# A streaming encoder layer on one core: where split weights start in their buffers, and the order of the opening's splits

## The chip, the cores and the metric

One core of a Trainium2 chip runs the whole layer in one launch. The metric is the device time in microseconds (us), the median of three runs. TensorE multiplies, VectorE and ScalarE do elementwise work, GpSimd small parts; DMA transfers are issued from an engine's queue, here nearly all from the sync engine (SP).

## The reference

One layer of a hybrid encoder over 2048 prompt tokens and 8 x 16 sample tokens, model width 1024, all in float32. Cut to what matters here:

```python
qm, km, vm, om, ip, fp, qa, ka, va = split_in(x @ w_in)          # input projection
hm = mlstm_chunkwise(...)                                        # 4 heads x 128
ha = swa_prompt(...) or swa_step(...)                            # windowed attention
mix = jnp.concatenate([hm, ha], axis=-1) @ w_out                 # output projection
h = layer_norm(DEEPNORM_ALPHA * x + mix, ln1_g, ln1_b)
u = h @ w_up                                                     # up product, 2 x 2816 wide
c = b_conv + sum(ext[:, j:j + T] * w_conv[j] for j in range(CONV_W))
a, g = jnp.split(c, 2, axis=-1)
y = layer_norm(DEEPNORM_ALPHA * h + (silu(g) * a) @ w_down, ln2_g, ln2_b)   # down product
```

## The kernel before, in words

Every large product is made in split precision: each operand is cast on ScalarE to a high part and the rest is subtracted on VectorE to a low part (`split`, L219: a cast at L221, a subtraction at L222). Three matmuls, high x high, high x low and low x high, then stand for one. The input, up and down products also use a seven-product scheme for 2 x 2 blocks: sums and differences of the quarters of weights and tokens are multiplied, products 1 to 7. The sums of tokens are called t1 to t4 in `x_steps` (L551), and a digit there is the split of that product's tokens.

The stages follow each other on TensorE. The input projection (`i_dense`, L599) goes over four blocks of 512 prompt tokens, the first with the sample tile beside it. `i_direct` (L735, matmuls at L747) makes keys, values and gates with narrow weights, `i_product` (L709, L721) one of the seven products for one of five groups of columns: 24 matmuls of 256 columns. In groups 0 and 1 the weights are the stationary operand and tokens move; in groups 2 to 4 the tokens are stationary and weights move. The sample tile's own products are at L731. The recurrence and the attention of finished blocks are woven between these matmuls as chains (`Chains`, L155 on). The output projection (`group`, L917, through `mm3`, L224 to L228) has tokens stationary and 512 columns of weights moving. The up product (`f_product`, L887, matmuls at L1895) has weights stationary and 384 or 320 tokens moving; the down product (`f_downs`, L2076, matmuls at L2103) has tokens stationary and 512 columns of weights moving.

The order on TensorE is written out by hand: `i_begin` (L346) lists the items of the input projection, and `i_dense` yields them with costs, by which the chains are woven in. For the first block the list begins with the gates of tiles 0 to 3, then product (block 0, group 0, 1), the gates of the sample tile, and (0,0,2), (0,1,1), (0,0,7), (0,0,6), (0,0,5), (0,0,4), (0,0,3). The other engines take their instructions in the order in which the program asks for them, with a priority for evictions.

Split weights stand in a ring of buffers: four with the tag `wlo`, four with `whi` (`WB = 4`), and two more, `wex`, from the second stage on. `half` (L398) gives one of them to the input and output projections, `f_slot` (L1782) to the up and down products. `advance` (L422) asks for as many splits (`next_split`, L472) and loads (`next_raw`, L431) as there are free buffers. A buffer's bytes in each partition begin where the pools put it: a pool lays its tiles out one after the other, each rounded up to 32 bytes, and a pool begins where the one before it ends. The largest tile of a tag sets the size of its buffers; the gates' tile of 2 x 2 x 272 floats makes it 4352 bytes, 17 x 256, for `wlo` and `whi`. `pad` (L216) takes some bytes of a pool to move what follows. By these sizes the first weight buffer begins at byte 1728, which is 192 past a multiple of 256, and all buffers of the ring do the same modulo 256, `wex` by its pad. Split tokens begin at a multiple of 256, and those of the down product, which `f_buf` (L1776) places 56 floats into their buffers, at 224 past one.

The opening is the part of `i_dense` ahead of its loop. It loads the tokens of block 0 in four quarters (`x_load`, L542; quarter 1 in two pieces), gate weights and the sample tile, all on the sync queue, warms TensorE up with products of zeros (`warm_up`, L326), then asks for the splits of gate weights and tokens. `x_steps(0, 1)` splits the first quarter in four pieces. Ahead of the loop it asks for all seven token operands of block 0 but product 4's.

## Time and profile before

| what | value |
| --- | --- |
| median of 3 runs | 2289.33 us (2288.55 to 2289.89) |
| profiled execution | 2291.27 us, its span 2289.5 us, mean granted TensorE clock 0.999 |
| instructions | 39775, of which 14293 matmuls |
| DMA | 631.30 MB, mean 276 GB/s |
| HBM | 457.02 MB read, 171.64 MB written |
| input projection, matmuls at L721 | first at 20.6 us, last at 613.6 us |
| output projection, L228 | 615.5 to 893.8 us |
| up product, L1895 | 894.2 to 1817.7 us |
| down product, L2103 | 1818.3 to 2280.7 us |

How to read it: the span runs from the first to the last instruction of one profiled execution. A row of the timeline gives start, length, engine, line, operation, output<-inputs and shapes; a matmul's inputs are named moving operand first, then the stationary one, and "x2" puts two that follow each other into one row. A matmul's length is drawn from its start to its modelled end, and matmuls are pipelined, so the distance between two starts is shorter than the length. The bracket at a row's end is the idle time of the engine before it and who ended it. Idle time of an engine other than the one that sets the end costs nothing.

### The profile page before, as it was taken

Reading aid. Unit: us, or ns where it says so; the run is one execution under the profiler, and the core shown is the slowest. Engines: PE = TensorE matmul, PEld = TensorE weight load, DVE = VectorE, ACT = ScalarE, POOL = GpSimd, SP = SyncE. Lnnn points to the kernel's source line nnn. Section 1 sums busy time; section 2 is a strip of 40 time slices with the busy share of each in tenths; the row PEclk is TensorE's granted clock in tenths of the full one; section 3 lists DMA queues with packets and bytes.
Section 4 is the critical chain, followed back from the end, with each engine's and each line's share of the span. In section 5 each row is a group of like instructions: output and inputs, shape, how many; then the busy total and the mean of one; then the engine's idle time right before and its main releaser. Section 6 shows DMA issues by size and latency. Waiting matters only on the chain. (4 is left out here: it accounts for less than half of the span.)

```text
span 2289.5 us, 39775 instructions
## 1 busy us (share of the span) xinstructions
PE 2269.4 (99%) x14293; PEld 2083.6 (91%) x14293; DVE 1808.9 (79%) x3068; ACT 1272.9 (56%) x2373; POOL 275.5 (12%) x509
## 2 busy tenths in 40 slices
PE   8999999999999999999999999999999999999998
PEld 8999999999878778999999999999999988888876
DVE  8787687777688888998778777778766786995987
ACT  5453476776766656555556555555555644444442
POOL 0001001000021110211112000113111200200200
PEclk9999999999999999999999999999999999999999
DMA  7989998899998867898778999988998786757752
GB/s 280 321 313 317 319 317 275 276 308 298 329 315 266 270 217 273 310 328 302 285 272 272 307 305 311 307 269 290 323 288 262 253 291 227 252 164 223 251 157 84
DMA packets 302133, 631.30 MB, mean 276 GB/s; under 512 B 47404, under 2 KB 140656, under 8 KB 301936
## 3 DMA queue, kind: packets, MB, share of 16 engines
q1 hardware_dynamic: 297264, 615.06, 79.5%
q0 software_dynamic: 3520, 10.56, 1.5%
q10 hardware_dynamic: 1152, 3.15, 0.4%
q8 instruction: 113, 1.85, 0.3%
q14 instruction: 84, 0.69, 0.1%
HBM read 457.02 MB, written 171.64 MB: 275 GB/s over the span
## 5 line engine op out<-in xcount | busy, mean ns | idle before, releaser
L1895 PE MATMUL fup<-hh,uw 128*128 128x384 f32 (+1 forms) x1848 | 476.9, 327 | 0.2 <-ACT ub L1924 0.2
L1895 PE MATMUL dps<-hh,uw 128*128 128x384 f32 (+1 forms) x1848 | 476.7, 327 | 0.0
L1895 PEld LDWEIGHTS fup<-hh,uw 128*128 128x128 f32 x1848 | 329.1, 188 | 0.5 <-ACT ub L1924 0.4
L1895 PEld LDWEIGHTS dps<-hh,uw 128*128 128x128 f32 x1848 | 329.1, 188 | 0.0
L1895 PE MATMUL fup<-hl,uw 128*128 128x384 f32 (+1 forms) x924 | 301.9, 327 | 1.0 <-DVE hl L222 1.0
L1895 PE MATMUL dps<-hl,uw 128*128 128x384 f32 (+1 forms) x924 | 301.6, 326 | 0.0
L1953 DVE SCALAR_TENSOR_TENSOR cc<-u,cw,cc 128x768 f32<-128x768 f32 (+1 forms) x264 | 258.0, 978 | 38.6 <-ACT cc L1951 30.2
L221 ACT CAST uw<-wraw 128x1024 fp32r<-128x1024 f32 x126 | 123.6, 981 | 229.0 <-PE dps L2103 122.5
L721 PE MATMUL dps<-w,oh 128*128 128x256 f32 x1344 | 250.3, 282 | 0.4 <-ACT dps L815 0.4
L222 DVE TENSOR_TENSOR w<-wraw,w 128x1024 fp32r<-128x1024 f32 (+2 forms) x163 | 186.1, 1149 | 61.8 <-ACT w L221 60.4
L221 ACT CAST w<-wraw 128x1024 fp32r<-128x1024 f32 (+2 forms) x163 | 160.3, 992 | 112.6 <-PE dps L721 58.3
L721 PEld LDWEIGHTS dps<-w,oh 128*128 128x128 f32 x1344 | 209.5, 188 | 11.5 <-issue 8.1
L222 DVE TENSOR_TENSOR uw<-wraw,uw 128x1024 fp32r<-128x1024 f32 x126 | 142.3, 1129 | 61.7 <-ACT uw L221 61.2
L721 PE MATMUL dps<-w,ol 128*128 128x256 f32 x672 | 186.8, 278 | 0.0
L1895 PEld LDWEIGHTS fup<-hl,uw 128*128 128x128 f32 x924 | 173.6, 188 | 1.7 <-DVE hl L222 1.6
L721 PE MATMUL dps<-oh,w 128*128 128x256 f32 x896 | 170.7, 284 | 3.8 <-DVE w L222 2.2
L2103 PE MATMUL fup<-uw,fu 128*128 128x512 f32 x726 | 173.8, 396 | 0.0
L1895 PEld LDWEIGHTS dps<-hl,uw 128*128 128x128 f32 x924 | 173.6, 188 | 0.0
L2103 PEld LDWEIGHTS fup<-uw,fu 128*128 128x128 f32 x726 | 136.4, 188 | 33.0
L2103 PE MATMUL dps<-uw,fu 128*128 128x512 f32 x660 | 165.0, 396 | 0.0
L2103 PEld LDWEIGHTS dps<-uw,fu 128*128 128x128 f32 x660 | 124.0, 188 | 30.0
L721 PEld LDWEIGHTS dps<-oh,w 128*128 128x128 f32 x896 | 140.5, 188 | 10.1 <-issue 4.1
(320 smaller groups left out, 4565.1 us busy)
## 6 DMA issues: line engine op xcount, KB each, us to landing
uw<-zw SPq DMA_DIRECT2D x176, 512.0 KB, 5.1
zw<-uw SPq DMA_DIRECT2D x88, 512.0 KB, 3.3
w<-zws SPq DMA_DIRECT2D x72, 512.0 KB, 6.3
wv<-wup SPq DMA_DIRECT2D x66, 512.0 KB, 5.4
wraw<-wi SPq DMA_DIRECT2D x65, 512.0 KB, 5.1
wraw<-zt SPq DMA_DIRECT2D x60, 512.0 KB, 4.6
wraw<-wdn SPq DMA_DIRECT2D x45, 512.0 KB, 4.9
wraw<-wo SPq DMA_DIRECT2D x40, 512.0 KB, 4.9
```

The costliest lines, as they stand in the source:

```text
L221: nc.scalar.copy(hi, src)
L222: return nc.vector.tensor_sub(lo, src, hi.bitcast(F32)).ins
L721: mm(o, l, r, start=s in (1, 7) and c == k == i == 0, stop=k == 3 and i == 2, skip_group_check=True)
L1895: mm(ps, l[:, k], r[:, k], start=s in (1, 7) and k == 0 and i == 0, stop=k == 3 and i == 2, skip_group_check=True)
L1953: V.scalar_tensor_tensor(c[:, v], u[:, i:i + n], w[i], c[:, v], op0=ALU.mult, op1=ALU.add)
L2103: mm(ps, l[:, k, c], r[:, k], start=s in (1, 4, 7) and u == 0 and k == 0 and i == 0, stop=u == nu - 1 and k == n - 1 and i == 2, skip_grou ...
```

## The change

It has two parts.

The first is where split weights begin. Every slot of the ring is now one tile of 1088 floats (`WS`, 4352 bytes), and the caller says at which float its data begin: `half(at, size)` and `f_slot(at)`. The offset is 16 floats (64 bytes) for groups 0 and 1 of the input projection, 48 floats (192 bytes) for groups 2 to 4 and for the up product, 0 for the gates, the output projection and the down product. A pad of 64 bytes in the first pool moves the ring's first buffer to byte 1792, a multiple of 256. The pads of the pools behind it are dropped, one of 192 bytes is added in `f_downs`, and `f_buf` is gone: the token buffers of the up and down products begin at their tiles' start, which by the sizes is again a multiple of 256.

The second is the opening's order. The load of the first raw gate weights and of token quarter 1 is asked for ahead of the warm-up; quarters 1 and 3 go in two pieces each and are issued from ScalarE's queue. The second token operand is split in two pieces, with a split of gate weights after each (`between`). Of the sums and splits of tokens only t3 and 7 stay ahead of the loop; t2 and 6 are asked for after the gates of the sample tile, t1 and 5 after product (0,0,2), t4, 4 and the sample tile's operand 4 after (0,1,1).

```diff
@@ -36,6 +36,7 @@
 
 WB = 4
 WR = 7
+WS = 1088
 
 
 IBLOCKS = [[0, 1, 2, 3, 16], [4, 5, 6, 7], [8, 9, 10, 11], [12, 13, 14, 15]]
@@ -248,11 +249,12 @@
             chains = Chains(self)
             self.xs, self.gates, self.i_done = {}, {}, 0
             self.i_begin()
+            self.next_raw()
+            self.x_load(0, 1)
             self.warm_up()
             chains.weave(self.i_dense())
             close(mcm)
             wx, wxcm = enter("wx1sb")
-            self.pad(wx, 192)
             self.unit_more(wx)
             self.mp, mcm = enter("osb")
             self.o_setup()
@@ -287,9 +289,7 @@
             close(xcm)
 
             self.wx, wxcm = enter("wx2sb")
-            self.pad(self.wx, 192)
             self.f2, f2cm = enter("f2sb")
-            self.pad(self.f2, 64)
             self.f3, f3cm = enter("f3sb")
             self.pad(self.f3, 192)
             self.pad(self.fp, 224)
@@ -310,6 +310,7 @@
         nc.vector.memset(self.eps, EPS)
         self.mhalf = cp.tile([P, 8], F32, name="mhalf")
         nc.vector.memset(self.mhalf, -0.5)
+        self.pad(cp, 64)
         self.zqk = [dp.tile([8, P, P * len(b)], F32, name=f"zqk{i}") for i, b in enumerate(IBLOCKS)]
         self.zws = [[dp.tile([1 if g < KEPT else 2, P, 4, HT], F32, name=f"zws{g}_{i}") for i in range(4)] for g in range(NG)]
         self.zo = [[dp.tile([len(b), P, 512], F32, name=f"{n}{i}") for i, b in enumerate(IBLOCKS)] for n in ("zqa", "zog", "zv")]
@@ -395,15 +396,15 @@
     def release(self, n):
         self.halves[1] += n
 
-    def half(self, shape):
+    def half(self, at, size):
         n = self.halves[0]
         self.halves[0] += 1
         if self.extra is not None:
             e = (n - self.extra) % (2 * WB + 2)
             if e < 2:
-                return self.wx.tile(shape, F32R, name="w", tag="wex", bufs=2)
+                return self.wx.tile([P, WS], F32R, name="w", tag="wex", bufs=2)[:, at:at + size]
         self.turn = 1 - self.turn
-        return self.wp.tile(shape, F32R, name="w", tag=("wlo", "whi")[self.turn], bufs=WB)
+        return self.wp.tile([P, WS], F32R, name="w", tag=("wlo", "whi")[self.turn], bufs=WB)[:, at:at + size]
 
     def unit_more(self, wx):
         self.wx, self.extra = wx, self.halves[0]
@@ -480,12 +481,13 @@
         self.us += 1
         if u[0] == "g":
             e = self.raw_of.pop(u)
-            w = self.half([P, 2, 2, 272])[:, :, :, :264]
+            w = self.half(0, WS).rearrange("p (i k m) -> p i k m", i=2, k=2)[:, :, :, :264]
             self.split(w[:, 0], w[:, 1], e[0])
             e[1] = True
             self.wu[u] = w[:, 0], w[:, 1]
             return True
-        hi, lo = self.half([P, 1024]), self.half([P, 1024])
+        at = 0 if u[0] == "o" else 16 if u[2] < 2 else 48
+        hi, lo = self.half(at, 1024), self.half(at, 1024)
         if self.kept(u):
             for i, t in enumerate((hi, lo)):
                 self.nc.sync.dma_start(t.bitcast(F32), self.zws[u[2]][SUMS.index(u[3])][i].rearrange("p a b -> p (a b)"))
@@ -543,12 +545,13 @@
         for q in qs:
             self.xr[b, q] = r = self.x_raw(q)
             x = self.a["xq"][b][(q - 1) // 2, (q - 1) % 2]
-            n = 2 if (b, q) == (0, 1) else 1
+            first = b == 0 and q in (1, 3)
+            n = 2 if first else 1
             for i in range(n):
                 k = slice(i * 4 // n, (i + 1) * 4 // n)
-                self.nc.sync.dma_start(r[:, k], x[:, k])
-
-    def x_steps(self, b, *steps):
+                (self.nc.scalar if first else self.nc.sync).dma_start(r[:, k], x[:, k])
+
+    def x_steps(self, b, *steps, between=None):
 
         nc, V = self.nc, self.nc.vector
         r = lambda q: self.xr[b, q]
@@ -571,11 +574,13 @@
                 x = self.xt[0] if s in (7, 6) else r({1: 1, 2: 3, 3: 4, "b12": 2, 5: 2, 4: 4}[s])
 
                 self.hx[b, s] = h, l = self.x_slot(4 if s == "b12" else s)
-                n = 4 if (b, s) == (0, 1) else 1
+                n = 4 if (b, s) == (0, 1) else 2 if (b, s) == (0, 2) else 1
                 for i in range(n):
                     k = slice(i * 4 // n, (i + 1) * 4 // n)
                     nc.scalar.copy(h[:, k], x[:, k])
                     V.tensor_sub(l[:, k], x[:, k], h[:, k].bitcast(F32))
+                    if between:
+                        between()
 
     def x_single(self, *steps):
@@ -601,8 +606,6 @@
         nb = len(IBLOCKS)
         last = NG - 1
 
-        self.next_raw()
-        self.x_load(0, 1)
         self.next_raw()
         self.x_load(0, 3)
         for _ in range(2):
@@ -617,16 +620,12 @@
         self.next_split()
         self.x_steps(0, 1)
         self.next_split()
-        self.x_steps(0, 2)
-        for _ in range(2):
-            self.next_split()
+        self.x_steps(0, 2, between=self.next_split)
         self.x_steps(0, "b12", 3)
         self.x_single(1, 2)
         self.next_raw()
         self.advance()
-        self.x_steps(0, "t3", 7, "t2", 6)
-        self.x_single(4)
-        self.x_steps(0, "t1", 5, "t4")
+        self.x_steps(0, "t3", 7)
         self.sb, self.trans = {}, None
 
         passages = [{1: ["load"], 7: ["t3", 7], 6: ["t2", 6], 2: [1], 5: [2], 3: [3, "t4"], 4: ["b12", "t1"]},
@@ -662,10 +661,11 @@
                 self.i_keys(b, ti, ps)
                 if ti == 3 and b or ti == 4:
                     self.release(4)
-                    self.x_steps(b, 4)
                     if b:
-                        self.x_steps(b, 5)
+                        self.x_steps(b, 4, 5)
                 self.advance()
+                if ti == 4:
+                    self.x_steps(0, "t2", 6)
                 continue
             _, b, g, s = item
             if item not in self.wu:
@@ -695,6 +695,11 @@
                 self.x_pair(0, (7, 5, 2, 3).index(s))
             with self.tc.issue_after(behind) if behind and b == 0 else nullcontext():
                 self.advance()
+            if (b, g, s) == (0, 0, 2):
+                self.x_steps(0, "t1", 5)
+            elif (b, g, s) == (0, 1, 1):
+                self.x_steps(0, "t4", 4)
+                self.x_single(4)
 
             if (b, g) in ((1, 1), (nb - 2, 1), (nb - 1, 0), (nb - 1, 2)):
@@ -1719,7 +1724,7 @@
 
             n = len(tiles) // 2
             for ts, tags in ((range(n), ("hh6", "hl6")), (range(n, 2 * n), ("hh7", "hl7"))):
-                w = [self.f_buf(fp, F32, "hst", tag, [3, 512]) for tag in tags]
+                w = [fp.tile([P, 3, 512], F32, name="hst", tag=tag, bufs=1) for tag in tags]
                 for c, t in enumerate(ts):
                     z = self.zh[tiles[t]].rearrange("p (i m) -> p i m", i=2)
                     at = [((2 * c + i) // 3, (2 * c + i) % 3) for i in range(2)]
@@ -1769,21 +1774,18 @@
                 V.tensor_sub(r3, r3, r2)
             else:
                 pool = self.fp if s in (1, 7, 6) else self.f3 if s == 4 else self.f2
-                hi, lo = [self.f_buf(pool, F32R, f"{n}{s}", f"{n}{s}", [4, 384]) for n in ("hh", "hl")]
+                hi = pool.tile([P, 4, 384], F32R, name=f"hh{s}", tag=f"hh{s}", bufs=1)
+                lo = pool.tile([P, 4, 384], F32R, name=f"hl{s}", tag=f"hl{s}", bufs=1)
                 self.split(hi[:, :, :h], lo[:, :, :h], src[s])
                 self.hc[b, s] = hi[:, :, :h], lo[:, :, :h]
 
-    def f_buf(self, pool, dt, name, tag, shape, at=0):
-
-        t = pool.tile([P, 1536 + (64 if pool is self.fp else 0)], dt, name=name, tag=tag, bufs=1)[:, at:at + 1536]
-        d = dict(zip("abc", shape[:-1]))
-        return t.rearrange(f"p ({' '.join(d)} m) -> p {' '.join(d)} m", **d)
-
-    def f_slot(self, dt=F32R):
+    def f_slot(self, at, dt=F32R):
         self.slot = (self.slot + 1) % 10
         if self.slot < 8:
-            return self.wp.tile([P, KD, P], dt, name="uw", tag=("whi", "wlo")[self.slot % 2], bufs=WB)
-        return self.wx.tile([P, KD, P], dt, name="uw", tag="wex", bufs=2)
+            w = self.wp.tile([P, WS], dt, name="uw", tag=("whi", "wlo")[self.slot % 2], bufs=WB)
+        else:
+            w = self.wx.tile([P, WS], dt, name="uw", tag="wex", bufs=2)
+        return w[:, at:at + D].rearrange("p (k m) -> p k m", k=KD)
 
     def f_raw(self, b, j):
@@ -1808,7 +1810,7 @@
                 self.f_raw(b, j)
             if b == 0:
                 v, g = self.wr[b, j]
-                s12, s34 = self.f_slot(F32), self.f_slot(F32)
+                s12, s34 = self.f_slot(48, F32), self.f_slot(48, F32)
                 V.tensor_add(s12[:, :4], g[:, :4], g[:, 4:])
                 V.tensor_sub(s34[:, :4], v[:, :4], g[:, :4])
                 V.tensor_sub(s12[:, 4:], s12[:, :4], v[:, :4])
@@ -1816,7 +1818,7 @@
                 self.wr[b, j] = v, g, s12, s34
         if s == 5 and (b, j) != (len(FBLOCKS) - 1, NFF - 1):
             self.f_raw(b + (j + 1) // NFF, (j + 1) % NFF)
-        w = self.f_slot().rearrange("p (i k) m -> p i k m", i=2)
+        w = self.f_slot(48).rearrange("p (i k) m -> p i k m", i=2)
         i = SUMS.index(s) if s in SUMS else None
         keep = None if i is None else self.zw[j][i].rearrange("p (i k m) -> p i k m", i=2, k=4)
         if b and i is not None:
@@ -2038,7 +2040,7 @@
         src = src[k0 + ks[0]:k0 + ks[-1] + 1, :, c0:c0 + 512].rearrange("k p n -> p k n")
         n = len(ks) * 512
         raw = self.wp.tile([P, 1024], F32, name="wraw", tag="wraw", bufs=WR)
-        hi, lo = [self.f_slot().rearrange("p a b -> p (a b)") for _ in range(2)]
+        hi, lo = [self.f_slot(0).rearrange("p a b -> p (a b)") for _ in range(2)]
         v = lambda t: t[:, :n].rearrange("p (a b) -> p a b", b=512)
         self.nc.sync.dma_start(v(raw), src)
         self.low = self.split(hi[:, :n], lo[:, :n], raw[:, :n])
@@ -2055,7 +2057,7 @@
         ks = slice(DUNITS[u][0], DUNITS[u][-1] + 1)
         n = len(DUNITS[u])
         r = {q: self.dr[b, q][:, ks, :h] for q in (1, 2, 3, 4) if (b, q) in self.dr}
-        w = self.f_buf(self.fp, F32R, "fu", ("hh1", "hl1", "hh7", "hl7", "hh6", "hl6")[self.ring % 6], [2, 2, 384], 56)
+        w = self.fp.tile([P, 2, 2, 384], F32R, name="fu", tag=("hh1", "hl1", "hh7", "hl7", "hh6", "hl6")[self.ring % 6], bufs=1)
         self.ring += 1
         if s == 6:
             V.tensor_sub(r[1], r[4], r[1])
@@ -2090,6 +2092,7 @@
         nb, nu = len(FBLOCKS), len(DUNITS)
         ys, ops = {}, {}
         last_tile = FBLOCKS[-1][0]
+        self.pad(self.wp, 192)
         st = self.wp.tile([P, 2, 6], F32, name="st", tag="st", bufs=1)
 
         def product(s, p, units):
```

## The prediction

> **What bounds the kernel now.** I read the page first, then the windows of the opening, the timeline of PE there, and last the timeline of PE stage by stage for the distance from one matmul's start to the next.
>
> ```profile
> span 2289.5 us, 39775 instructions
> PE 2269.4 (99%) x14293; PEld 2083.6 (91%) x14293; DVE 1808.9 (79%) x3068; ACT 1272.9 (56%) x2373; POOL 275.5 (12%) x509
> ```
>
> TensorE is busy for 2269.4 of 2289.5 us and its instructions stand in an order written out by hand. So there are two things to win: the 20.1 us in which it is idle, and the distance between matmuls that follow each other without a gap. The second isn't in the busy time (a matmul is drawn longer than its distance to the next); it is read from starts. The change aims at both: the opening's order at the first, the byte offsets at the second.
>
> ```profile
> 0.00:6.00 6.00, 4.02 (x10) 3.13 (x10) 2.99 (x13) 2.63 (x4) 0.31 (x5) 1.00 0.60 176
> 6.00:18.70 12.70, 11.28 (x82) 10.48 (x81) 9.31 (x17) 8.21 (x17) 0.00 (x0) 1.00 1.03 408
> 18.70:50.00 31.30, 28.40 (x234) 27.59 (x233) 31.12 (x53) 16.16 (x26) 0.00 (x0) 1.00 0.72 249
> ```
>
> These are windows of the opening (stretch, length, busy PE, PEld, DVE, ACT, POOL, then clock, DMA share, GB/s). Until 6 us the DMA engines are busy for only 0.60 of the time; then they are full to 18.7 us (1.03, 408 GB/s); from there to 50 us VectorE works 31.12 of 31.30 us. First the loads, then VectorE, set the pace.
>
> ```profile
> 8.28 0.39 PE L747 MATMUL dps<-w,oh 128*128 128x264 f32 x1 [0.73 <-ACT w L221]
> 9.02 0.39 PE L747 MATMUL dps<-w,oh 128*128 128x264 f32 x1 [0.36 <-DVE w L222]
> ...
> 11.81 0.39 PE L747 MATMUL dps<-w,oh 128*128 128x264 f32 x1 [0.34 <-DVE w L222]
> ...
> 33.66 0.50 PE L721 MATMUL dps<-oh,w 128*128 128x256 f32 x2 [1.30 <-DVE w L222]
> ...
> 41.83 0.50 PE L721 MATMUL dps<-oh,w 128*128 128x256 f32 x2 [0.91 <-DVE w L222]
> ...
> 45.37 0.39 PE L721 MATMUL dps<-oh,w 128*128 128x256 f32 x1 [0.69 <-ACT zev L787]
> ```
>
> These are PE's idle times in the opening after its first real product (the bracket is the idle time and who ended it): 0.73 + 0.36 + 0.34 = 1.4 us for the first splits, 1.30 + 0.91 = 2.2 us for weight splits of VectorE, 0.69 us for an eviction.
>
> **The change, the opening.** VectorE's queue ahead of the wait that ends at 33.66 us:
>
> ```profile
> 23.90 1.22 DVE L569 TENSOR_TENSOR xr<-xr 128x1024 f32<-128x1024 f32 x1
> ...
> 27.44 1.22 DVE L578 TENSOR_TENSOR ol<-xr,oh 128x1024 fp32r<-128x1024 f32 x1
> ...
> 29.92 1.22 DVE L565 TENSOR_TENSOR xr<-xr,xt 128x1024 f32<-128x1024 f32 x1
> ...
> 32.39 1.22 DVE L222 TENSOR_TENSOR w<-wraw,w 128x1024 fp32r<-128x1024 f32 x1
> ```
>
> The split at 32.39 is the one that PE waits for (it ends at 33.6). Ahead of it stand the sum t1 (23.90), the split of tokens 5 (27.44) and the sum t4 (29.92), all for products (0,0,5) to (0,0,4), which come after the product that waits. The change asks for t1 and 5 after product (0,0,2), for t4 and 4 after (0,1,1), and for t2 and 6 after the single tile: 3 x 1.22 = 3.7 us leave the queue ahead of the split, t2 and 6 perhaps too. The wait is 1.30 us, so it goes, and I take the 0.91 us at 41.83 to go as well: there the same three steps are still ahead less t4, some 2.4 us, and PE comes 1.3 us earlier. What is late next is the deferred work itself: t1, 5, t4 and 4 are 4 x 1.22 = 4.9 us, to be done between (0,1,1) and (0,0,4), while VectorE has no idle time to give. Their cover is the queue of split weights that stands ahead of PE (four units of two halves); gone, it costs at most the 2.2 us that were won. The 0.69 us stays: product (0,0,5) needs the bank that (0,0,6) has just filled.
>
> The loads of tokens 1 and 3 go in halves by ScalarE's queue, so the sync queue has three issues fewer ahead of the gate weights and the first weights (the halves of 1, and 3 whole). Below 6 us the DMA engines have 0.40 of their time free, 2.4 us of full rate; what is issued earlier there also lands earlier. Bounds for the 1.4 us of first waits: all of it, and nothing if the landing of the first tokens stays put; the free 2.4 us exceed it, so I take it all. The four issues lie on ScalarE, which before its first cast does a table load alone and then sits idle until tokens land; they are covered there, and if they aren't, the first cast is late by what sticks out. Tokens 2 in two pieces cost two more small operations, covered by VectorE's idle time from 6 to 18.7 us (9.31 busy of 12.70). Opening: 3.6 us won, between 0 and 5.
>
> **The change, the offsets.** From the tile sizes in the code (each rounded up to 32 bytes): before, all split weights stand at 192 bytes past a multiple of 256, split tokens at 0, and tokens of the down product at 224. After, weights stand at 64 in groups 0 and 1 of the input projection, at 192 in groups 2 to 4 and in the up product, and at 0 in the gates, the output projection and the down product, whose tokens come to 0. The other tokens stay at 0. So the address pairs change in groups 0 and 1 (weights stationary, 192 to 64), in the output projection (moving weights, 192 to 0) and in the down product (stationary 224 to 0, moving 192 to 0); groups 2 to 4 and the whole up product keep theirs. Does a pair of offsets set the distance?
>
> ```profile
> 178.18 0.40 PE L721 MATMUL dps<-oh,w 128*128 128x256 f32 x2
> ...
> 181.00 0.40 PE L721 MATMUL dps<-oh,w 128*128 128x256 f32 x2
> ```
> ```profile
> 118.12 0.39 PE L721 MATMUL dps<-w,oh 128*128 128x256 f32 x2
> ...
> 120.16 0.39 PE L721 MATMUL dps<-w,oh 128*128 128x256 f32 x2
> ```
> ```profile
> 227.28 0.40 PE L721 MATMUL dps<-w,oh 128*128 128x256 f32 x2
> ...
> 232.23 0.40 PE L721 MATMUL dps<-w,oh 128*128 128x256 f32 x2
> ```
> ```profile
> 116.53 1.52 PE L731 MATMUL psx<-w,xs 128*128 128x256 f32 x12
> 117.89 0.28 PE L721 MATMUL dps<-w,oh 128*128 128x256 f32 x1
> ...
> 120.62 1.58 PE L731 MATMUL psx<-w,xs 128*128 128x256 f32 x12
> 122.03 0.28 PE L721 MATMUL dps<-w,oh 128*128 128x256 f32 x1
> ```
>
> Each row is a run of matmuls by its start; the moving operand is named first. Groups 0 and 1 (weights stationary at 192, tokens moving at 0): 24 matmuls in 2.82 us, 117.5 ns. Groups 2 to 4 (tokens stationary at 0, weights moving at 192): 18 in 2.04 us, 113.3 ns; but elsewhere 42 in 4.95 us, 117.9 ns, with the same offsets. The sample tile's products, with the same moving weights, have the stationary tile at 128 in the first (12 in 1.36 us, 113.3 ns) and at 64 in the second (12 in 1.41 us, 117.5 ns). So there are two paces, 4 ns apart; the stationary address tips the choice, though it doesn't fix it.
>
> The Trainium skill (TensorE: Matmul & The Clock Gate, step 1 of "What happens when you issue a matmul") says that weights are loaded through a read port of their own and take nothing from the running matmul; by that no offset matters and this part of the sum would be 0. The two rows of the sample tile speak against it.
>
> What 64 against 0 gives isn't in the trace. Ends: the slow pace stays (0), or all is at 113.3.
>
> ```profile
> L721 PE MATMUL dps<-w,ol 128*128 128x256 f32 x672 | 186.8, 278 | 0.0
> ...
> L721 PE MATMUL dps<-oh,w 128*128 128x256 f32 x896 | 170.7, 284 | 3.8 <-DVE w L222 2.2 <-ACT mr L1172 0.9 <-ACT zev L787 0.7
> ...
> L721 PE MATMUL dps<-ol,w 128*128 128x256 f32 x448 | 125.1, 279 | 0.0
> ```
>
> Groups 0 and 1 are 896 + 448 = 1344 matmuls: at most 1344 x 4.2 ns = 5.6 us. In groups 2 to 4 the stationary operand stands 64 past the moving one (modulo 256), as the changed groups will; by the nearest row (672 matmuls of mean 278, between the 276 of the fast pace and the 280 of the slow) they run at half of each. I take the middle: 1344 x 2.4 ns = 3.2 us.
>
> The long products:
>
> ```profile
> 775.78 0.39 PE L228 MATMUL dps<-w,ol 128*128 128x512 f32 x1
> ...
> 777.18 0.39 PE L228 MATMUL dps<-w,ol 128*128 128x512 f32 x1
> ```
> ```profile
> 1959.66 1.56 PE L2103 MATMUL dps<-uw,fu 128*128 128x512 f32 x6
> 1961.06 1.56 PE L2103 MATMUL fup<-uw,fu 128*128 128x512 f32 x6
> ```
>
> The output projection (stationary at 0) makes 6 matmuls in 1.40 us, the down product (stationary at 224) 6 in 1.40 us: 233.3 ns each, whatever the stationary address. So I take 0 for both. But moving weights stood at 192 in both; 0 is untried at this length.
>
> ```profile
> 162.06 0.40 PE L747 MATMUL dps<-w,oh 128*128 128x264 f32 x2
> ...
> 162.42 0.41 PE L747 MATMUL dps<-w,oh 128*128 128x264 f32 x2
> ...
> 162.79 0.40 PE L747 MATMUL dps<-w,oh 128*128 128x264 f32 x2
> ```
> ```profile
> L226 PE MATMUL dps<-w,oh 128*128 128x512 f32 x272 | 114.1, 420 | 0.0
> ```
> ```profile
> L2103 PE MATMUL fup<-uw,fu 128*128 128x512 f32 x726 | 173.8, 396 | 0.0
> ...
> L2103 PE MATMUL dps<-uw,fu 128*128 128x512 f32 x660 | 165.0, 396 | 0.0
> ...
> L2103 PE MATMUL fht<-uw,fu 128*128 128x512 f32 x594 | 146.2, 396 | 0.2 <-DVE yacc L2134 0.2
> ```
>
> In the gate products the moving rows start in turn at 192/64 and 0/128, and three matmuls take 0.36 and 0.37 us in turn: some 3 ns apart per matmul. The projection has 3 x 272 = 816 long matmuls, the down product 726 + 660 + 594 = 1980, together 2796: 3 ns either way is 8.4 us.
>
> **The sum.** 3.6 + 3.2 = 6.8 us off the span of 2289.5. The profiled execution took 2291.27 us and the median of the runs is 2289.33; taken off the median that is 2282.5 us.
>
> **The rivals.** (a) The long products gain too: 6.8 + 8.4 = 15.2 us, 2274 us. For it: the gate rows, where the address of the moving operand shows. Against it: the same 233.3 ns in two stages. 0.2. (b) The offsets do nothing, since the pace is chosen by something that 64 doesn't touch (the same offsets gave 113.3 and 117.9): 3.6 us, 2285.7 us, within 0.2%. 0.17. By the rule of the Trainium skill named above (TensorE: Matmul & The Clock Gate) it would end here too. (c) VectorE's wait comes back at the deferred splits: 2.2 us less, 2284.7 us. 0.05. (d) Slower: moving weights at 0 fall in with the stationary tokens at 0, both streams starting at the same place, and each long matmul takes 5 ns more (the gap of the two paces, rounded up): 2796 x 5 = 14 us against 6.8, 2296.5 us. It is slower than now from 2.4 ns on. For it: no row shows 0 against 0 at 512 columns. Against it: the gate rows have the stationary tile at 0 too and are not slower at 0. 0.08. My forecast, all of the opening and some of the groups, has 0.5.
>
> **How the numbers follow.** About 0.2% (4.6 us) is what a measurement of this kernel can tell from no change. Faster: the forecast and (a), 0.7. Same: (b) and (c), 0.22. Slower: (d), 0.08. The range of the forecast alone is 0 to 5 us from the opening and 0 to 5.6 from the groups, 2279 to 2288; it is taken down to 2271 for (a) with all of the opening and most of the groups. What is left out is (d) and the far ends.
>
> **What would show it.** The opening: PE's waits at L721 for VectorE's split fall from 2.2 us to under 0.5, those at L747 from 1.4 to under 0.5, and the first input product starts some 1.4 us earlier. The groups: runs of 24 matmuls with moving tokens take 2.72 us in places, not 2.82, and the mean of the 448 falls from 279 towards 278. The long ones: six in 1.40 us as before. I am wrong if six take 1.38 or less (a) or 1.43 or more (d), if every run of 24 in groups 0 and 1 still takes 2.82 us, or if new waits of VectorE stand between 38 and 60 us.

## The result, and the profile after

| | before | after |
| --- | --- | --- |
| median of 5 runs | 2289.33 us (2288.55 to 2290.69) | 2270.28 us (2269.26 to 2271.05) |
| profiled execution, its span | 2291.27, 2289.5 us | 2269.26, 2267.5 us |

The changed kernel takes 0.9914 of the time (95% interval 0.9901 to 0.9928): 19.05 us less, where 6.8 were forecast. The profiled execution of before lies 1.9 us above its median and that of after 1.0 us below, so the two spans differ by 22.0 us.

The page of after, answering to the two lines quoted first in the prediction:

```profile
span 2267.5 us, 39785 instructions
PE 2249.1 (99%) x14293; PEld 2079.8 (92%) x14293; DVE 1807.5 (80%) x3069; ACT 1273.4 (56%) x2374; POOL 269.7 (12%) x509
```

TensorE's busy time fell by 20.3 us with the same 14293 matmuls, its idle time only from 20.1 to 18.4 us. So most of the gain isn't idle time removed: the matmuls follow each other at a shorter distance, and this does show in the busy time, of which the prediction said that the distance isn't in it. Where, is read from the source view: per line and operand pair the count, the lengths (least/median/most, ns), and the first and last start (us). Of the kernel before, one row from each stage:

```profile
L721 PE MATMUL dps<-w,oh x1344: 276/276/467, 71.6 to 613.6; 128*128 128x256 f32 x192
L721 PE MATMUL dps<-oh,w x896: 276/279/471, 20.6 to 527.9; 128*128 128x256 f32 x180
...
L228 PE MATMUL dps<-w,ol x272: 390/394/401, 615.5 to 893.8; 128*128 128x512 f32 x136
L1895 PE MATMUL dps<-hh,uw x1848: 304/336/423, 905.4 to 1817.7; 128*128 128x384 f32 x124, 128*128 128x320 f32 x61
L2103 PE MATMUL fht<-uw,fu x594: 392/396/500, 1887.6 to 2280.7; 128*128 128x512 f32 x198
```

The same rows of the kernel after (its L229 is L228 of before), with one more of the output projection, L228, whose row before, at L227, had a median of 394:

```profile
L726 PE MATMUL dps<-w,oh x1344: 276/276/467, 68.7 to 607.9; 128*128 128x256 f32 x192
L726 PE MATMUL dps<-oh,w x896: 276/276/470, 20.4 to 522.3; 128*128 128x256 f32 x180
...
L228 PE MATMUL dps<-w,oh x272: 387/389/402, 609.6 to 884.6; 128*128 128x512 f32 x136
L229 PE MATMUL dps<-w,ol x272: 388/392/401, 609.9 to 884.9; 128*128 128x512 f32 x136
L1897 PE MATMUL dps<-hh,uw x1848: 304/336/423, 896.7 to 1808.5; 128*128 128x384 f32 x124, 128*128 128x320 f32 x61
L2106 PE MATMUL fht<-uw,fu x594: 388/389/505, 1876.4 to 2258.8; 128*128 128x512 f32 x198
```

The last starts give the lead at the end of each stage: input projection 613.6 - 607.9 = 5.7 us (0.2 of it at its first product, 20.6 against 20.4), output projection 893.8 - 884.9 = 8.9, up product 1817.7 - 1808.5 = 9.2, down product 2280.7 - 2258.8 = 21.9. So the output projection gave 3.2 us, the up product 0.3, whose offsets did not change, and the down product 12.7. The medians say the same: 396 to 389 ns in the down product, 279 to 276 in groups 0 and 1 (stationary `w`), 336 in the up product both times.

As in the prediction, the pace is the distance between starts. The timeline of after, first in the output projection, then in the down product:

```profile
768.83 0.39 PE L227 MATMUL dps<-w,oh 128*128 128x512 f32 x1
...
770.20 1.03 PE L1366 MATMUL ppt<-ident,sc 128*128 128x128 f32 x8
...
1960.26 1.52 PE L2106 MATMUL fup<-uw,fu 128*128 128x512 f32 x6
1961.62 2.66 PE L2106 MATMUL dps<-uw,fu 128*128 128x512 f32 x11
```

Six matmuls of 512 columns lie between each pair: 1.37 and 1.36 us, where before both stages took 1.40.

PE's idle times in the opening after its first real product:

```profile
7.39 0.39 PE L752 MATMUL dps<-w,oh 128*128 128x264 f32 x1 [0.31 <-ACT w L222]
8.13 0.39 PE L752 MATMUL dps<-w,oh 128*128 128x264 f32 x1 [0.35 <-DVE w L223]
14.46 0.52 PE L752 MATMUL dps<-w,oh 128*128 128x264 f32 x2 [0.81 <-ACT gates L761]
32.15 0.39 PE L726 MATMUL dps<-oh,w 128*128 128x256 f32 x1 [0.38 <-ACT zev L784]
42.72 0.39 PE L726 MATMUL dps<-oh,w 128*128 128x256 f32 x1 [0.69 <-ACT zev L792]
47.44 0.38 PE L726 MATMUL dps<-oh,w 128*128 128x256 f32 x1 [0.20 <-DVE zev L796]
```

The two waits for VectorE's weight split (2.2 us) are gone and the first waits fell from 1.4 to 0.7 us. In their place stands a wait of 0.81 us for an eviction, of which ScalarE's own rows tell the cause:

```profile
12.93 1.14 ACT L594 CAST xs<-xsr 128x512 fp32r<-128x512 f32 x2 [0.20 <-DMA xsr<-xs]
13.98 0.36 ACT L760 COPY zev<-dps 128x256 f32<-128x256 f32 x1
14.24 0.17 ACT L761 COPY gates<-dps 128x8 f32<-128x8 f32 x1
```

The evictions at 13.98 and 14.24 us stand behind two casts of the sample tile, which themselves waited 0.20 us for their tile to land.

### The profile page after: what moved, and what is told of

Its sections match the earlier page's. It is cut to its first block, busy times and chain, and to the rows that moved or that the text cites. A ratio compares the mean times of both kernels' runs of the same rounds, so it can differ in the third digit from the quotient of the medians.

```text
span 2267.5 us, 39785 instructions
## 1 busy us (share of the span) xinstructions
PE 2249.1 (99%) x14293; PEld 2079.8 (92%) x14293; DVE 1807.5 (80%) x3069; ACT 1273.4 (56%) x2374; POOL 269.7 (12%) x509
## 4 chain that ended last, share of the span: by engine, by line
PE 82%; DVE 4%; ACT 1%; issue 1%; DMA 0%; POOL 0%; DVEq 0%; SPq 0%; ACTq 0%; POOLq 0%
PE dps L1897 20%; PE fup L1897 20%; PE dps L726 8%; PE fup L2106 7%; PE dps L2106 7%; PE fht L2106 6%; PE dps L227 2%; PE dps L229 2%; PE dps L228 2%; PE ppo L1372 1%; PE ppt L1366 1%; PE psc L1327 1%; DVE w L223 1%; PE fht L1719 1%; PE dps L752 1%
## 5 line engine op out<-in xcount | busy, mean ns | idle before, releaser
L2106 PE MATMUL fup<-uw,fu 128*128 128x512 f32 x726 | 169.0, 389 | 0.0
```

What stands on the lines that cost most here:

```text
L2106: mm(ps, l[:, k, c], r[:, k], start=s in (1, 4, 7) and u == 0 and k == 0 and i == 0, stop=u == nu - 1 and k == n - 1 and i == 2, skip_grou ...
```

## The experiments

Theories were formed from this result. To name them: the *distance* of a stage is the start of its stationary operand less that of its moving operand, modulo 256 bytes. Before, it was 192 in groups 0 and 1, 64 in groups 2 to 4, 64 in the output projection, 192 in the up product and 32 in the down product; after, 64, 64, 0, 192 and 0. All shares below compare a run with the kernel before timed beside it on the same chip.

**The down product: which address counts.** Three kernels differ from the changed one in the down product alone.

```diff
 # down_w192_t0: weights (moving) at 192, tokens (stationary) at 0
-        hi, lo = [self.f_slot(0).rearrange("p a b -> p (a b)") for _ in range(2)]
+        hi, lo = [self.f_slot(48).rearrange("p a b -> p (a b)") for _ in range(2)]
 # down_w192_t192: that, and the tokens at 192; down_w0_t224: weights at 0, tokens at 224 (56 floats)
-        w = self.fp.tile([P, 2, 2, 384], F32R, name="fu", ...)
+        w = self.fp.tile([P, 1600], F32R, name="fu", ...)[:, 48:48 + 1536].rearrange(...)
```

> The changed kernel with one offset put back: the down product's weights start at 192 past a multiple of 256 again, its tokens stay at 0. Theory 1 (a long matmul's pace is set by where its moving operand starts modulo 256): the 1980 matmuls of the down product fall back from 226.7 to 233.3 ns, six in 1.40 us, and the kernel loses 1980 x 6.67 ns = 13.2 us of the 19.1 won, some 2283.5 us. Theory 2 (what counts is the distance from the stationary start to the moving one, 0 in the changed kernel): the same here, since the distance becomes 64, at which the output projection ran at 233.3 before. Theory 3 (the stationary tokens' move from 224 to 0 was what helped): no change, 2270 us.

> The changed kernel with the down product's weights and tokens both at 192: distance 0 as in the changed kernel, but the moving operand at 192. Theory 1 (place of the moving operand): 233.3 ns a matmul, about 2283.5 us. Theory 2 (distance): 226.7 ns, about 2270 us. One look at the pace tells them apart.

> The changed kernel with the down product's tokens alone put back to 224, weights at 0. Theory 1 (place of the moving operand): 226.7 ns a matmul as in the changed kernel, about 2270 us. Theory 2 (distance of the two starts): the distance is 224 and no longer 0, so 233.3 ns, about 2283.5 us. Theory 3 (place of the stationary operand): 233.3 ns.

One row of the source view of each, in this order:

```profile
L2106 PE MATMUL fup<-uw,fu x726: 393/396/399, 1808.6 to 2177.9; 128*128 128x512 f32 x182
```
```profile
L2106 PE MATMUL fup<-uw,fu x726: 388/389/398, 1811.0 to 2170.2; 128*128 128x512 f32 x182
```
```profile
L2106 PE MATMUL fup<-uw,fu x726: 393/396/398, 1810.9 to 2180.3; 128*128 128x512 f32 x182
```

With the weights alone at 192 (distance 64) the median is 396 again and the time 2282.37 us (0.9971, interval 0.996 to 0.9982): 7.0 us below the kernel before instead of 19.05, so the stage is worth 12.1 us. With both at 192 (distance 0) it is 389 and 2271.2 us (one run). With the weights left at 0 and the tokens at 224 it is 396 and 2283.8 us (one run). So it is not the place of the moving operand, nor of the stationary one: of the three theories only the distance fits all four kernels, and 192 with 192 is as good as 0 with 0 (226.8 and 226.7 ns from start to start).

**The opening alone.** The offsets of the changed kernel with the opening of the kernel before (the diff is shown in part: the loads' queue and pieces and the later requests go back too).

```diff
-            self.next_raw()
-            self.x_load(0, 1)
             self.warm_up()
...
-        self.x_steps(0, 2, between=self.next_split)
+        self.x_steps(0, 2)
+        for _ in range(2):
+            self.next_split()
...
-        self.x_steps(0, "t3", 7)
+        self.x_steps(0, "t3", 7, "t2", 6)
+        self.x_single(4)
+        self.x_steps(0, "t1", 5, "t4")
```

> The changed kernel with its opening put back: loads by the sync queue, warm-up first, all token sums asked for ahead of the loop. By the timelines of the two kernels the start of the 300th matmul is 2.65 us earlier after the change, so this one loses 2.6 us: 2272.9 us, with waits of 1.30 and 0.91 us for weight splits back at 33 and 42 us. Rival: the opening's gain is taken up by later waits of the chains or of splits, and the time stays at 2270.3 within 1 us.

It took 2273.03 us (0.9928, interval 0.9915 to 0.994), 16.33 us below the kernel before: the opening is worth 2.7 us. VectorE's waits are back:

```profile
34.36 0.50 PE L721 MATMUL dps<-oh,w 128*128 128x256 f32 x2 [1.51 <-DVE w L223]
42.52 0.51 PE L721 MATMUL dps<-oh,w 128*128 128x256 f32 x2 [1.00 <-DVE w L223]
```

**The loads on ScalarE's queue.** The changed order, with all loads of the first tokens on the sync queue.

```diff
-                (self.nc.scalar if first else self.nc.sync).dma_start(r[:, k], x[:, k])
+                self.nc.sync.dma_start(r[:, k], x[:, k])
```

> The changed kernel with the order kept, but token quarters 1 and 3 issued from the sync queue again. Theory A (the order of splits makes the opening's gain; the earlier loads are given back when TensorE waits 0.81 us at 14.46 us for an eviction behind ScalarE's casts): the first waits are longer, up to 1.4 us behind at the 40th matmul, but level with the changed kernel within 0.4 us at the 300th. Theory B (the loads by a second queue matter): at the 300th matmul it is 1 us or more behind, and so is the time.

One run took 2270.59 us, 18.57 below its own before. Its first wait is longer than after's 0.31 us, and further on it waits for a split of tokens:

```profile
8.40 0.39 PE L752 MATMUL dps<-w,oh 128*128 128x264 f32 x1 [0.89 <-ACT w L222]
...
39.07 0.39 PE L726 MATMUL dps<-ol,w 128*128 128x256 f32 x1 [0.63 <-DVE ol L581]
```

The split that ends this wait is that of tokens 6, one of the deferred ones. Yet at the 301st matmul nothing of this is to be seen. The order of the matmuls is the same in all these kernels, so the start of the same matmul can be compared. Counted from the first gate product, by starts in the trace, each kernel leads the kernel before by (us):

| kernel | 41st | 61st | 221st | 301st |
| --- | --- | --- | --- | --- |
| after | 1.21 | 0.14 | 1.28 | 2.65 |
| opening_before | -0.71 | -0.69 | -0.70 | -0.53 |
| opening_sync | 0.48 | 0.50 | 2.27 | 2.81 |
| third_bank (below) | 1.34 | 1.35 | 1.50 | 2.95 |

The changed kernel wins 1.2 us up to the 41st matmul and loses nearly all of it in the wait of 0.81 us, which by starts costs 1.07; the kernel without ScalarE's loads wins 0.5, keeps it, and stands at the same place at the 301st. How far single executions scatter is seen in the four kernels that differ from the changed one only behind the input projection (down_w192_t0, down_w192_t192, down_w0_t224 and out_before below): they lead by 0.9 to 1.5 us at the 41st matmul, by 0.3 to 0.5 at the 61st and by 2.7 to 3.1 at the 301st. So the loss before the 61st is real, and no lasting gain of ScalarE's queue is seen.

**Groups 0 and 1, and the output projection.** One offset back each.

```diff
-        at = 0 if u[0] == "o" else 16 if u[2] < 2 else 48
+        at = 0 if u[0] == "o" else 48 if u[2] < 2 else 48      # groups_before
+        at = 48 if u[0] == "o" else 16 if u[2] < 2 else 48     # out_before
```

> The new kernel with the weights of groups 0 and 1 back at 192 bytes (distance 192 instead of 64), all else new. If the stage's time in the trace (3.0 us) is the truth: 3 us slower than the new kernel, 2273.3 us, and the pace of its 1344 matmuls 117.6 instead of 115.1 ns. If the distance isn't what moved this stage (the opening's order could have): 2270.3 and 115.1 ns.

> The new kernel with the moving weights of the output projection back at 192 bytes (distance 64 instead of 0), all else new. If the stage's time in the trace is the truth: 816 matmuls x (233.3 - 229.0) = 3.5 us slower, 2273.5 us. If the sum of the timed runs is (4.2 for both stages, 3.3 of it in the groups): 1 us slower, 2271.3 us.

groups_before took 2272.88 us (0.9925, interval 0.9913 to 0.9938), out_before 2272.8 (0.9927, interval 0.9914 to 0.9939). Against their common before (2289.73) these are 16.85 and 16.93 us, so the groups are worth 2.2 us and the output projection 2.1. The medians went back with the offsets, to 279 (276 in the changed kernel) in the one and to 394 at L228 (389) in the other:

```profile
L726 PE MATMUL dps<-oh,w x896: 276/279/471, 20.9 to 525.2; 128*128 128x256 f32 x180
```
```profile
L228 PE MATMUL dps<-w,oh x272: 388/394/398, 611.1 to 888.2; 128*128 128x512 f32 x136
```

Together: 12.1 + 2.7 + 2.2 + 2.1 = 19.1 us, the whole of the 19.05. Each share has the uncertainty of its run's interval, some 3 us either way, so that the sum closes this well is partly luck. That each share is there at all is safer: every run of the four kernels with one part put back was slower than every run of the changed kernel, and the paces went back with the offsets, to 117.6 instead of 115.2 ns in the one, 233.1 instead of 229.0 in the other (how they are worked out stands below). By paces and starts the shares are larger, 13.1 + 2.7 + 3.2 + 3.3 = 22.3 us; that is the difference of the two profiled spans, not that of the medians.

**What distance is best at what length.** Six kernels, each with other offsets in every stage; one run each. The edits are the numbers in `half`'s `at` and in the calls of `f_slot`, as here for scan_a:

```diff
-        at = 0 if u[0] == "o" else 16 if u[2] < 2 else 48
+        at = 16 if u[0] == "o" else 0 if u[2] < 2 else 0
-                s12, s34 = self.f_slot(48, F32), self.f_slot(48, F32)
+                s12, s34 = self.f_slot(0, F32), self.f_slot(0, F32)
-        w = self.f_slot(48).rearrange("p (i k) m -> p i k m", i=2)
+        w = self.f_slot(0).rearrange("p (i k) m -> p i k m", i=2)
-        hi, lo = [self.f_slot(0).rearrange("p a b -> p (a b)") for _ in range(2)]
+        hi, lo = [self.f_slot(16).rearrange("p a b -> p (a b)") for _ in range(2)]
```

> The changed kernel with other offsets in every stage; distance is stationary start less moving start, modulo 256. Groups 0 and 1: 0 (was 64). Groups 2 to 4: 0 (was 64). Up product: 0 (was 192). Output projection and down product: 192 (was 0). Distance theory, from what is shown so far (0 is the good place at 512 columns; 32, 64 and 224 cost 6.7 ns): the two long products at 233.3 ns a matmul, 16 to 19 us lost there. For the up product and the groups it says only that the pace may move with the distance: if 0 is good at every length, the up product falls from 173.3 towards 166.7 ns (25 us won over 3696 matmuls of 384 columns) and the groups keep to 113.3. Rival (the good distance differs with the number of columns): the up product stays at 173.3 or gets slower, and the groups go to 117.5 or more.

> As the first scan with other distances. Groups 0 and 1: 128 (stationary 128, moving 0). Groups 2 to 4: 192 (stationary 0, moving 64). Up product: 64. Output projection and down product: 128. Distance theory: the long products at 233.3 ns or worse; the groups at 192 run at the slow 117.5 as groups 0 and 1 did before at 192, and those at 128 at 118.2 as the sample tile's products did at 128. Rival (the stationary start alone sets the groups' pace, 0 and 128 good, 64 and 192 bad): groups 0 and 1 at 128 and groups 2 to 4 at 0 both mostly at 113.3.

> As the first scan with other distances. Groups 0 and 1 back at 192, as before the change: a mean of 117.5 ns and not 115.1, some 3 us lost there. Groups 2 to 4: 128 (stationary 0, moving 128): by the distance theory slow, by the rival of the stationary start as before. Up product: 128. Output projection: 96, down product: 160; both at 233.3 ns or worse by the distance theory.

> Distances (stationary start less moving start, modulo 256) off the multiples of 64: groups 0/1 and groups 2-4 of the input projection 48, output projection 240, up product 224, down product 16. Theory G (granule: only multiples of 64 can escape, any other distance pays the dear pace): 512 columns 233.3 ns in both long products, 256 columns some 119.8, up product 176 ns at 384; about 12 + 3 + 10 + 12.5 = 38 us above the new kernel, some 2308 us. Theory N (near is good enough: the pace changes smoothly with the distance): 512 columns 226.7 to 228, 256 columns 115, 384 columns 173.3; within 5 us of 2270.

> Distances: groups 0/1 and 2-4 80, output projection 16, up product 32, down product 240. Theory G: 512 columns 233.3 ns, 256 columns 119.8, 384 columns 176, some 2308 us as in the run before. Theory N: groups as at 64 (115 ns), long products 226.7 to 229, up product 173.3 to 175, 2270 to 2278 us. A third outcome, a pace below 226.7 at 512 or below 173.3 at 384, would mean that the changed kernel has not the best distance.

> Distances: groups 0/1 96, groups 2-4 32, output projection 8, up product 240, down product 248. Theory G: as the two before, some 2308 us; 8 bytes are enough to lose the good pace of distance 0 (233.3 instead of 226.7 at 512 columns). Theory N: 8 bytes from 0 cost nothing, both long products at 226.7; groups between 115 and 119.

They took 2286.71, 2294.29, 2303.77, 2299.09, 2293.36 and 2298.39 us, a to f. One row of each of three stages of scan_a, where the groups and the up product stand at distance 0 and the down product at 192:

```profile
L726 PE MATMUL dps<-oh,w x896: 276/283/472, 20.2 to 533.1; 128*128 128x256 f32 x180
L1897 PE MATMUL fup<-hh,uw x1848: 306/334/423, 897.8 to 1814.7; 128*128 128x384 f32 x124, 128*128 128x320 f32 x61
L2106 PE MATMUL fup<-uw,fu x726: 388/392/398, 1822.3 to 2184.9; 128*128 128x512 f32 x182
```

Distance 0 is bad for the groups (283 against 276), costs the up product nothing (173.4 against 173.3 ns in the table below; its drawn length is even 2 ns less), and 192 costs the down product 3 ns of the 7 by drawn length, 2.3 of the 6.6 by pace, where the expectation had the whole. The pace by distance, in ns, is the mean distance between starts of neighbours of one stage and shape, worked out from the starts of all kernels; gaps 20% or more above the median are left out as waits. Where several kernels have the same distance they agree within 0.2 ns, in groups 2 to 4 within 0.5:

| columns (stage) | 0 | 8 | 16 | 32 | 48 | 64 | 80 | 96 | 128 | 160 | 192 | 224 | 240 | 248 |
| --- | --- | --- | --- | --- | --- | --- | --- | --- | --- | --- | --- | --- | --- | --- |
| 512, down | 226.7 | | 234.3 | 233.3 | | 233.3 | | | 232.7 | 233.3 | 229.0 | 233.3 | 231.7 | 233.1 |
| 512, output | 229.0 | 232.6 | 235.3 | | | 233.1 | | 233.8 | 232.6 | | 229.5 | | 231.7 | |
| 384, up | 173.4 | | | 173.4 | | 175.0 | | | 176.0 | | 173.3 | 174.7 | 175.3 | |
| 256, groups 0/1 | 119.7 | | | | 118.4 | 115.2 | 118.7 | 117.9 | 118.7 | | 117.6 | | | |
| 256, groups 2-4 | 119.8 | | | 118.3 | 118.8 | 115.1 | 119.3 | | 118.9 | | 116.3 | | | |

No distance is best for all lengths: 0 at 512 columns, 64 at 256 (and 0 the worst there), while at 384 columns 0, 32 and 192 are equal. At 512 and 256 columns a place off the multiples of 64 never reached the best pace; 8 bytes beside 0 (248) cost the down product 6.4 of the 6.6 ns. So neither a smooth curve nor a granule of 64 alone describes it: at 384 columns 32 is as good as 0. The stationary start alone doesn't set the pace either: it was 0 in groups 2 to 4 in every kernel, at 115.1 to 119.8 ns. The changed kernel has, in each stage, a distance as good as any of those tried, and no better version came out of the scan.

Two of the means hide more than one pace. In groups 0 and 1 of the changed kernel, all at distance 64, one stretch makes 18 matmuls in 2.04 us (113.3 ns) and another 18 in 2.12 (117.8):

```profile
64.80 0.39 PE L726 MATMUL dps<-oh,w 128*128 128x256 f32 x2
...
66.84 0.39 PE L726 MATMUL dps<-oh,w 128*128 128x256 f32 x2
```
```profile
176.83 0.40 PE L726 MATMUL dps<-oh,w 128*128 128x256 f32 x2
...
178.95 0.40 PE L726 MATMUL dps<-oh,w 128*128 128x256 f32 x2
```

So at 256 columns the distance shifts how often the faster pace is met and doesn't fix the pace of each matmul (in the table the two rows at 192 lie 1.3 ns apart); what chooses in a stretch was not found. In the output projection, 229.0 ns where the down product has 226.7 at the same distance, the runs of matmuls are broken by those of the attention. In the run that begins at 633.78 us, six starts from 634.09 on take 1.39 us and the next six 1.36.

**The eviction's wait.** Two kernels were to take away the 0.81 us.

```diff
 # keys_first
-        self.x_single(1, 2)
         self.next_raw()
...
                     self.i_keys(b, 1, self.ib[2])
+                    self.x_single(1, 2)
 # third_bank
-                ps = self.bank([P, 512], "pg") if ti == 4 else self.ib[ti % 2 * 2]
+                ps = self.bank([P, 512], "pg") if ti == 4 else self.ib[1 if (b, ti) == (0, 2) else ti % 2 * 2]
```

> The new kernel with the casts and differences of the sample tile (tokens 1 and 2 of it) asked for after the evictions of the first two tiles' gate products. Theory E (the eviction's place in ScalarE's queue takes the gain of the early loads back): the wait of 0.81 us at 14.46 us goes, the lead over the kernel before at the 60th matmul rises from 0.2 to some 1.0 us, and of that up to 0.8 us is left at the end: 2269.5 us. Theory V (VectorE sets the pace from 18.7 us on, so what is won before it is given back at the waits near 32 to 48 us): the wait goes, the lead rises, and the time stays at 2270.3.

keys_first took 2270.7 us (0.9923, interval 0.991 to 0.9937), but tells nothing: its ScalarE rows show both casts of the sample tile still ahead of the evictions, though the program asks for them later, and the wait was still there (0.97 us). So ScalarE's order isn't always the order of asking that the section on the kernel gives it.

```profile
12.87 1.14 ACT L594 CAST xs<-xsr 128x512 fp32r<-128x512 f32 x2 [0.20 <-DMA xsr<-xs]
13.91 0.37 ACT L760 COPY zev<-dps 128x256 f32<-128x256 f32 x1
14.18 0.17 ACT L761 COPY gates<-dps 128x8 f32<-128x8 f32 x1
```

> The new kernel with the gate products of the third tile written to the third bank, which stands empty, instead of the first, which has to be evicted; every engine's order is the same. The wait of 0.81 us near 14.4 us should go in any case. Theory E (the wait takes the gain of the early loads back): the lead over the kernel before at the 60th matmul is 1.0 us instead of 0.2, and at the 300th 3.5 us instead of 2.7: 2269.5 us. Theory V (splits and evictions on VectorE and ScalarE set the pace from 18 to 55 us): a lead of 1.0 us at the 60th and still 2.7 us at the 300th, with waits of PE between 30 and 50 us longer by the same amount: 2270.3 us.

third_bank gives other values in its first output, so it is no version to use; the matmuls, their shapes and their order are those of the changed kernel. It took 2270.93 us (0.9919, interval 0.9905 to 0.9932). PE's idle times in it:

```profile
7.29 0.39 PE L752 MATMUL dps<-w,oh 128*128 128x264 f32 x1 [0.32 <-ACT w L222]
8.04 0.39 PE L752 MATMUL dps<-w,oh 128*128 128x264 f32 x1 [0.35 <-DVE w L223]
31.92 0.39 PE L726 MATMUL dps<-oh,w 128*128 128x256 f32 x1 [1.16 <-ACT zev L784]
42.50 0.39 PE L726 MATMUL dps<-oh,w 128*128 128x256 f32 x1 [0.69 <-ACT zev L792]
47.22 0.38 PE L726 MATMUL dps<-oh,w 128*128 128x256 f32 x1 [0.29 <-DVE zev L796]
```

The wait near 14 us is gone and the lead at the 61st matmul is 1.35 us instead of 0.14. But the next wait, for an eviction near 32 us, grew from 0.38 to 1.16 us, and the 2.95 us at the 301st matmul are no more than what the changed kernel and the four others with its opening and its wait have there (2.65 to 3.09). ScalarE's rows tell who sets this wait, first in the changed kernel, then in third_bank:

```profile
30.56 1.05 ACT L222 CAST w<-wraw 128x1024 fp32r<-128x1024 f32 x1 [1.68 <-DVE wraw L520]
31.52 0.57 ACT L784 COPY zev<-dps 128x512 f32<-128x512 f32 x1
```
```profile
30.34 1.05 ACT L222 CAST w<-wraw 128x1024 fp32r<-128x1024 f32 x1 [2.50 <-DVE wraw L520]
```

The eviction stands behind a cast that waits for a sum of weights on VectorE, which from 18.7 to 50 us is busy for 31.02 of 31.30 us in third_bank. What is won early makes ScalarE wait longer for VectorE, and so is taken back, as theory V had it.

## Why the prediction was wrong

- **The long products: the step that failed.** The prediction took 0 for them, because both stages ran at 233.3 ns "whatever the stationary address". They measured 12.1 us (down) and 2.1 (output projection; 3.2 by the traces). The row was read rightly, but it holds two distances, 64 and 32, and the table shows that these two cost the same; the distance that the change goes to, 0, was in neither. The step compared stationary addresses, at one moving address, and took the absence of a difference for the absence of an effect, though for the groups the prediction had itself gone by how far the one operand stands past the other. That "0 is untried at this length" was said, and then left at 0 in the sum.
- **Its rival (a)** was the case. Its size was 2796 x 3 ns = 8.4 us, from the gate rows; measured are 1980 x 6.6 = 13.1 us by pace in the down product and 816 x 4.1 = 3.3 in the projection. The 3 ns were too small, and no measure of this length: they were read from two steps of 0.36 and 0.37 us at another length (over 48 such pairs of the kernel before the two steps differ by 3 ns, 1 ns per matmul), and the table has the effect with another sign at 256 columns. That (a) came out is in part luck: its reason, the moving operand's address, was not what decided.
- **Rival (d)**, equal starts colliding, has the sign wrong at 512 columns, where equal starts are the best. At 256 columns it would have been right in kind: distance 0 gives 119.7 ns, the slowest of those tried.
- **Groups 0 and 1**: 3.2 us forecast, 2.2 measured by the undoing, and by pace 1344 x 2.4 = 3.2 us (117.6 to 115.2). The step held: the nearest row, groups 2 to 4, had the same distance of 64 and both now have its pace of some 115 ns, as a mix of the two paces that the prediction named. The sign held too: 18 matmuls in 2.04 us are 24 in 2.72.
- **The opening**: 3.6 forecast, 2.7 measured; the difference is less than the uncertainty of the runs, so the terms are judged by the traces. VectorE's 2.2 us of waits went as forecast. The 1.4 us of first waits, taken whole, did not last: half of them is still there as the two waits of 0.31 and 0.35, the first input product starts 0.2 us earlier and not 1.4, and what was won went into the eviction behind the sample tile's casts. The prediction looked for what is late next on VectorE, and it was first ScalarE's order; third_bank shows that without this wait VectorE's work takes the gain, by way of the next eviction.
- **Rival (c)**: in the changed kernel no deferred split became late, and of new waits for VectorE between 38 and 60 us there is one of 0.20. Its mechanism is real, though: with the loads on the sync queue a deferred split cost 0.63 us.
- **Rival (b)** fell in every stage whose distance changed, though "something that 64 doesn't touch" is there: the two paces at one distance. The rule of the Trainium skill named beside it (TensorE: Matmul & The Clock Gate, step 1 of "What happens when you issue a matmul"), by which loading the next weights takes no read bandwidth from the running matmul, doesn't agree with these runs as far as it would make the places of the two operands indifferent: 226.7 against 233.3 ns by the distance of their starts alone.

One slip in the working changes little: nothing from the opening and nothing from the groups would be 2289.3 us, not the 2288 that ends the forecast's own range.

What stays open is the mechanism. The runs show that the pace depends on the distance of the two starts and on the length of the product; that nothing but the distance counts is shown for one case alone, 0 with 0 against 192 with 192 at 512 columns. They don't show which reads meet, why 64 is good at 256 columns and 0 at 512, nor what chooses between the two paces at 256.

## What to carry to other kernels

Where a long row of matmuls loads a new stationary operand for each, time a few distances of the two operands' starts for each length (0, 64 and 192 modulo 256 first): in this kernel the best and the worst of those tried lie nearly 4% of a matmul apart at 512 and 256 columns, 1.5% at 384 and nothing at 320, for a few bytes of padding. Compare pairs, not single addresses; two rows with one pace say nothing of a third pair. And a stall removed early in a pipeline pays only as far as the next supplier has slack: look for the next wait on every engine, evictions included, and for what these wait for themselves, before counting it.

## What the runs showed of the hardware that was not expected

- The same 1980 matmuls of 512 columns, same instructions and order, run at 226.7 or 233.3 ns by the distance of the operands' starts; 192 with 192 is as good as 0 with 0, and 8 bytes of distance already cost 6.4 ns.
- At 256 columns matmuls with the same starts modulo 256 keep to 113.3 ns in one stretch and to 117.8 in another.
- The up product's 320-column matmuls did not care: a mean of 146.7 ns at every distance tried.
- Four loads issued from ScalarE's queue held that engine for 1.86 us and moved its table load from 0.74 to 2.63 us, as its rows in the changed kernel show. The kernel with these loads on the sync queue had its table load at 0.74 and still the longer first wait (0.89 against 0.31 us):

```profile
0.74 1.86 ACTq L552 DMA_DIRECT2D xr<-xq  x4
2.63 1.28 ACT L222 ACT_TABLE_LOAD   x1 [2.63 <-issue]
```
```profile
0.74 1.28 ACT L222 ACT_TABLE_LOAD   x1 [0.74 <-PEq L2215]
```
